# Wide items of 512 columns for v and the first head's q and k, and one weighing for the first four query tiles of a head

## The chip, the cores and the metric

The kernel runs on one core of one Trainium2 chip. The metric is the device time of one execution in microseconds (us); a time is the median of several runs. Five engines work side by side on the core and wait for each other by semaphores: TensorE (PE in the profile; PEld is its weight load), VectorE (DVE), ScalarE (ACT), GpSimd (POOL) and SyncE (SP), whose queue here does nothing but start DMAs. Each engine takes its instructions in the order in which they stand.

## The reference

One decoder layer on 1024 tokens of width 1024, in float32:

```python
h = rms_norm(x, attn_norm_w[l])
proj = h @ w_in[l]
q, k, v, u, g = jnp.split(proj, splits, axis=-1)
# per head: two 64-wide halves of q and k, QK-norm, relative-position bias, causal softmax
p = probs(qb1, k1f) - lamf * probs(qb2, k2f)
return jnp.einsum('bhqk,bhkd->bhqd', p, vf)
# then: per-head norm, convolution branch of width 31 on u, two gated projections,
# x = x + m @ w_out;  x = x + SwiGLU(rms_norm(x))
```

The 8 heads have 128 columns of v each and 128 columns of q and of k each (two halves of 64).

## The kernel before, in words

**Matmuls.** Every float32 product is made of two float32r parts, `hi` (a rounded copy, made by ACT) and `lo` (the remainder, made by DVE or POOL). `mm3` issues three matmuls: hi x hi, hi x lo, lo x hi. A matmul has 128 rows of weights and moves 128, 256, 384 or 512 columns past them; its result lies in PSUM, whose banks hold 512 float32 columns.

**The first stage** (generator `first_stage`) normalises and turns x into `hT_hi`, `hT_lo`, and runs items of the input projection:
- the opening with the first 256 columns of v (V0) and the first convolution chunk U0;
- `first`: V1 and V2, 256 columns of v each. `v_item` takes the weights in two halves of 512 rows (`ld_wide`) and, for a pair of token tiles, fills the two halves of one bank with 24 matmuls of 256 columns each (`gemm_N`);
- seven pairs of convolution chunks (`u_pair`), whose weight sums and token sums POOL prepares;
- `last`: Q0 (q and k of head 0, 128 columns each) and V3 (the last 256 columns of v). `q_item` copies each bank to `qkraw` with ACT, sums the squares of 16 pieces of 64 columns (8 ACT instructions for a bank), makes 1/rms on DVE, scales, and leaves for later (`late`) the turning: PE transposes into a bank pQ, ACT and DVE make the parts `ks`, `klo`, `qs`, and DMAs copy halves of 64 partitions (`turn_qk`).

In the background DVE works through the convolution taps (31 for a chunk, `conv_taps`); ACT makes the first tap of a chunk, copies the finished sum out of PSUM (`done`), and SP writes it to DRAM. `done` and the sums of the chunks 4 to 7 (`acc`) take turns in one buffer of SBUF.

**Attention.** 64 steps (head, query tile) in the order 4, 5, 6, 7, 0, 1, 2, 3 within a head, the last head apart. A step computes scores and softmax (`scores`), turns the weights of the step before into `ph`, `pl` (`turn`), and every second step weighs the values of two query tiles with them (`weigh`, 256 columns in bank pW): for the tiles 2b and 2b+1, 2b+2 key tiles of three matmuls. `back` turns the result. Between them lie pieces of the fill: the items Q1 to Q7 (256 columns) and G0 to G15 (512 columns).

**What sets the order.** The code names what must come after what; within that, a scheduler that simulates the program lays down each engine's order when the kernel is built. So another width of one item moves instructions of all engines around it. The weights come through one stream (`ws`): `ahead` says how many loads are fetched in front. Its split tiles `whi`, `wlo` have three buffers each, the raw tiles `wraw` two. During the first stage `pg` has four banks, in attention two.

Of the kernel before, what the change touches and what calls it, by code (L numbers as in the profile page):

```python
# [13 lines left out]
ALU = mybir.AluOpType  # L14
# [43 lines left out]
def kernel(  # L58
# [284 lines left out]

    class Stream:
# [57 lines left out]
    first = ["V1", "V2"]  # L402
    last = ["Q0", "V3"]
# [12 lines left out]
    def loads_of(it):  # L416
        c = int(it[1:])
        if it[0] == "V":
            return ld_wide(win, [(V0 + 256 * c, 256)])
        if it[0] == "Q":  # L420
            return ld_wide(win, [(Q0 + c * P, P), (K0 + c * P, P)])
        if it[0] == "U":
# [339 lines left out]
    def bias_rows(c0):  # L762
# [6 lines left out]
        pool.dma_start(oh, buckets[:, c0 : c0 + 384])  # L769
# [3 lines left out]
        pool.dma_start(b_d[:, c0 : c0 + 384], gr)  # L773
# [11 lines left out]

    def q_item(h):
        halves = [ws.next(), ws.next()]
        t = {}
        T[h] = t
        for b in (1, 0):  # L790
# [14 lines left out]
            r = rstd_of(ss[:], 16, 1.0 / HD, fast=h > 0)  # L805
            r4 = raw[:].rearrange("p i (g d) -> p (i g) d", d=HD)
            dve.tensor_tensor(r4, r4, r.unsqueeze(2).to_broadcast([P, 16, HD]), op=ALU.mult)

            def turn_qk(z, key, b, raw):


                dma = nc.sync.dma_start
                pt = pm("pQ")
                for i in range(4):
                    pe.transpose(pt[:, i * P : (i + 1) * P], raw[:, i, z * P : (z + 1) * P], ident[:])  # L815
                w = pcol(key + "n")

                def part(j):
                    return qkp.tile([P, 512], F32R, tag=f"{key}s{j}", name=f"{key}s{j}_{h}_{b}", bufs=2 if key == "q" else 3)

                s1, s2 = part(1), part(2)
                act.activation(s1[:], pt[:], AF.Identity, scale=w)
                lo = part(3) if key == "q" else qkp.tile([P, 512], F32R, tag="klo", name=f"klo_{h}_{b}", bufs=1)
                dve.scalar_tensor_tensor(lo[:], pt[:], w, f32(s1[:]), op0=ALU.mult, op1=ALU.subtract)
                if key == "q":
                    dma(f32(s2[HD:, :]), f32(s1[HD:, :]))
                    lo2 = part(4)
                    for one, two in ((s1, s2), (lo, lo2)):
                        if one is lo:
                            dma(f32(two[HD:, :]), f32(one[HD:, :]))  # L830
                        dma(f32(two[:HD, :]), f32(one[HD:, :]))
                        dma(f32(one[HD:, :]), f32(one[:HD, :]))
                    t["q", b] = (s1, lo), (s2, lo2)
                else:
                    act.activation(s2[HD:, :], pt[HD:, :], AF.Identity, scale=w[HD:, :])
                    dma(f32(s2[:HD, :]), f32(lo[HD:, :]))
                    dma(f32(s1[HD:, :]), f32(lo[:HD, :]))
                    t["k", b] = s1, s2

            for z, key in ((1, "k"), (0, "q")):
                free = NT * (h - 1) + (0 if key == "k" and b else NT if key == "q" and not b else NT // 2)
                late.append((free if h else 0, lambda a_=(z, key, b, raw): turn_qk(*a_)))
# [3 lines left out]
    MAKE = {"V": v_item, "U": u_item, "Q": q_item, "G": g_item}  # L848

# [179 lines left out]
    def first_stage():  # L1029
# [13 lines left out]
        for n, _ in enumerate(run(first)):  # L1043
            if n < 5:
                tsum.pop(0)()
            if n == 2:
                ws.ahead = 1
                ws.fetch()
                ws.ahead = 0
# [1085 lines left out]
```

## Time and profile before

| | |
|---|---|
| median of 3 runs | 1727.08 us (1726.94 to 1728.37) |
| span of the profiled execution | 1725.7 us, 25863 instructions |
| busy: PE, PEld | 1714.6 us (99%), 1477.9 us (86%) |
| busy: DVE, ACT, POOL | 1275.4 us (74%), 862.5 us (50%), 219.1 us (13%) |
| V1 and V2 on PE | from 65.27 us to 111.78 us |
| Q0 and V3 begin on PE; first score of attention | 242.67 us; 306.78 us |

The profiled execution has no time of its own beside its span; the median of the runs lies 1.4 us above that span. In rows of groups, "busy" is the time in which at least one of the group's instructions ran, "mean" the duration of one, and matmuls overlap, so the distance from one start to the next is shorter than the duration. The rows of a timeline begin with the start and the duration in us.

### The profile page before, as it was taken

How to read it: one execution, taken by the hardware profiler on the slowest of the kernel's cores; microseconds unless marked ns; L12 is line 12 of the kernel's file. 1: busy time of each engine (PE TensorE's matmuls, PEld its weight loads, DVE VectorE, ACT ScalarE, POOL GpSimd, SP SyncE). 2: the span in 40 equal slices, each digit the busy share in tenths (PEclk: the TensorE clock that was granted, in tenths of full speed). 3: DMA queues.
4: the chain of work that ended last, by engine and by line, in shares of the span. 5: the costliest groups of instructions: out<-in, count | busy, mean ns of one | idle time of the engine just before them, and what ended most of it. 6: DMA issues, size and time to landing. Idle time of an engine off the chain costs nothing.

```text
span 1725.7 us, 25863 instructions
## 1 busy us (share of the span) xinstructions
PE 1714.6 (99%) x9243; PEld 1477.9 (86%) x9243; DVE 1275.4 (74%) x2128; ACT 862.5 (50%) x1958; POOL 219.1 (13%) x207
## 2 busy tenths in 40 slices
PE   9999999999999999999999999999999999999999
PEld 7997889998998998988788888888888888888887
DVE  7675889898988888878687769966676666575544
ACT  5333335767777776756556325633333333333332
POOL 3997851000000000000000000000000000000000
PEclk9999999999999999999999999999999999999999
DMA  6344445336345344343973683245455445598663
GB/s 208 116 126 132 131 151 154 104 109 171 104 127 147 115 125 138 101 136 130 333 238 118 200 296 119 74 135 164 147 170 170 154 141 164 175 355 285 217 215 130
DMA packets 261604, 281.64 MB, mean 163 GB/s; under 512 B 16546, under 2 KB 181986, under 8 KB 261475
## 3 DMA queue, kind: packets, MB, share of 16 engines
q1 hardware_dynamic: 254160, 267.71, 48.3%
q0 software_dynamic: 5680, 9.39, 2.6%
q10 hardware_dynamic: 1634, 2.89, 0.5%
q8 instruction: 73, 1.20, 0.3%
q14 instruction: 57, 0.46, 0.1%
HBM read 181.84 MB, written 85.50 MB: 155 GB/s over the span
## 4 chain that ended last, share of the span: by engine, by line
PE 92%; DMA 3%; DVE 2%; ACT 1%; issue 1%; POOL 0%; SPq 0%; DVEq 0%; POOLq 0%; ACTq 0%
PE acc L980 29%; PE acc L488 12%; PE pg L168 12%; PE pg L169 12%; PE pg L170 12%; PE wo L1850 3%; PE sc L1290 2%; PE sc L1289 2%; PE pT L1328 2%; PE pg L1106 1%; DVE acc L594 1%; PE pW L168 1%; PE pW L169 1%; PE pW L170 1%; PE pQ L815 1%
## 5 line engine op out<-in xcount | busy, mean ns | idle before, releaser
L594 DVE SCALAR_TENSOR_TENSOR acc<-u,cw,acc 128x1023 f32<-128x1023 f32 (+14 forms) x240 | 303.4, 1264 | 23.2 <-ACT acc L588 20.7
L170 PE MATMUL pg<-whi,hT_lo 128*128 128x256 f32 x704 | 200.2, 285 | 0.0
L168 PE MATMUL pg<-whi,hT_hi 128*128 128x256 f32 x704 | 199.7, 285 | 0.4 <-DVE v L125 0.4
L169 PE MATMUL pg<-wlo,hT_hi 128*128 128x256 f32 x704 | 199.5, 284 | 0.0
L125 DVE TENSOR_TENSOR wlo<-draw,whi 128x1024 fp32r<-128x1024 f32 x75 | 91.7, 1223 | 83.4 <-ACT whi L120 78.9
L120 ACT CAST whi<-draw 128x1024 fp32r<-128x1024 f32 x75 | 79.1, 1055 | 129.5 <-PE acc L488 114.3
L169 PEld LDWEIGHTS pg<-wlo,hT_hi 128*128 128x128 f32 x704 | 134.4, 191 | 1.8
L170 PEld LDWEIGHTS pg<-whi,hT_lo 128*128 128x128 f32 x704 | 134.3, 191 | 1.8
L168 PEld LDWEIGHTS pg<-whi,hT_hi 128*128 128x128 f32 x704 | 134.0, 191 | 2.1 <-DVE v L125 0.6
L120 ACT CAST whi<-wraw 128x1024 fp32r<-128x1024 f32 x90 | 94.7, 1052 | 70.6 <-PE pg L169 32.6
L488 PE MATMUL acc<-wlo,whi 128*128 128x512 f32 x308 | 119.8, 389 | 0.0
L488 PE MATMUL acc<-whi,wlo 128*128 128x512 f32 x308 | 119.8, 389 | 0.0
L1296 ACT ACTIVATE E<-E,mn 128x640 f32<-128x640 f32 (+7 forms) x128 | 99.8, 781 | 30.8 <-DVE mn L1291 29.2
L168 PE MATMUL pg<-hT_hi,whi 128*128 128x512 f32 x288 | 114.4, 397 | 0.1
L169 PE MATMUL pg<-hT_lo,whi 128*128 128x512 f32 x288 | 113.7, 395 | 0.0
L170 PE MATMUL pg<-hT_hi,wlo 128*128 128x512 f32 x288 | 113.7, 395 | 0.0
L120 ACT CAST whi<-s 128x1024 fp32r<-128x1024 f32 x54 | 56.9, 1053 | 104.9 <-PE acc L980 101.8
L125 DVE TENSOR_TENSOR wlo<-wraw,whi 128x1024 fp32r<-128x1024 f32 x75 | 93.3, 1246 | 12.6 <-ACT whi L120 12.3
L1291 DVE CUSTOM_DVE_ANT_0 E<-sc,tb 128x512 f32<-128x512 f32 (+3 forms) x128 | 74.2, 585 | 33.2 <-PE pT L1328 16.1
L980 PE MATMUL acc<-h_hi,whi 128*128 128x512 f32 x240 | 93.4, 389 | 0.0
L980 PE MATMUL acc<-h_lo,whi 128*128 128x512 f32 x240 | 93.4, 389 | 0.0
L980 PE MATMUL acc<-h_hi,wlo 128*128 128x512 f32 x240 | 90.1, 389 | 0.0
(370 smaller groups left out, 4589.7 us busy)
## 6 DMA issues: line engine op xcount, KB each, us to landing
wraw<-in_w_gate_up_dram SPq DMA_DIRECT2D x44, 512.0 KB, 4.7
wraw<-in_w_in_dram SPq DMA_DIRECT2D x38, 512.0 KB, 4.0
qs<-qs SPq DMA_DIRECT2D x96, 128.0 KB, 2.3
wd<-in_w_down_dram SPq DMA_DIRECT2D x44, 256.0 KB, 3.1
tdT<-wd SPq DMA_DIRECT2D x88, 128.0 KB, 4.8
draw<-sdS SPq DMA_DIRECT2D x44, 256.0 KB, 3.7
draw<-tdT SPq DMA_DIRECT2D x44, 256.0 KB, 3.7
wraw<-in_w_in_dram SPq DMA_DIRECT2D x32, 256.0 KB, 3.3
```

The lines of the kernel that those rows point to most:

```text
L120: act.copy(dst, src)
L125: last_lo[0] = dve.tensor_tensor(dst, src, f32(hi), op=ALU.subtract).ins
L168: pe.matmul(o, lh, rh, start=start, stop=False)
L169: pe.matmul(o, lh, rl, start=False, stop=False)
L170: last_mm[0] = pe.matmul(o, ll, rh, start=False, stop=stop).ins
L488: m = pe.matmul(o[s_][i][:], l_[:, ts], r_[:, 512:], start=start and j + y_ == 0, stop=j == n - 1 and y_ == 2, skip_group_check=not start,)
L594: dve.scalar_tensor_tensor(a_, us[c][:, : S - n], cw[:, c, t : t + 1], a_, op0=ALU.mult, op1=ALU.add)
L980: last_mm[0] = pe.matmul(o[:], a_[x_][:, k, :], b_[y_][:, k, :], start=start and k + x_ + y_ == 0, stop=k == 3 and x_ == 1, skip_group_che ...
L1289: pe.matmul(o[:, :w], qh[:, qs], k, start=True, stop=False)
L1291: dve.tensor_tensor_reduce(e[:, ks], o[:, :w], tb[:, S - nk + c0 : S - nk + c0 + w], 1.0, mn[:, j : j + 1] if c0 else 3.0e38, ALU.add, ALU ...
L1296: act.activation(e[:, :nk], e[:, :nk], AF.Exp, bias=mn[:, j : j + 1], scale=-1.0, accum_out=l[:, j : j + 1])
L1850: last_mm[0] = pe.matmul(o[s_][i][:], A[u_], B[v_], start=start and j + y_ == 0, stop=j == 3 and y_ == 2, skip_group_check=not start,).ins
```

## The change

V1 and V2 become one item W1 of 512 columns of v; Q0 and V3 become one item W0 of 128 columns of q, 128 of k and 256 of v. A wide item takes its weights in quarters of 256 rows (`ld_quarters`), in the order 0, 1, 2, 3, 0: for four token tiles it holds four banks and goes through the quarters 0 to 3; for the other four through 1, 2, 3, and 0, which is loaded again. Each of the four tiles is taken from its bank after the last quarter. W0 works on the tokens 512 to 1023 first.

In heads 0 to 6 the four query tiles 0 to 3 share one pair `ph`, `pl` with 512 columns, and one `weigh` handles them after tile 3: key tile k for the columns from 128k on, so three matmuls each of 512, 384, 256 and 128 columns in place of 18 of 256. The buffers of `ph` and `pl` are no longer zeroed for these tiles.

The splits of W1's weights go to DVE up to the sixth step (before, POOL took those of V2), and the six DMAs of `bias_rows` go from POOL's queue to SP's.

```diff
+    def ld_quarters(w, cols):
+        def quarter(g):
+            def go():
+                raw = wraw()
+                r3 = raw[:].rearrange("p (k c) -> p k c", c=512)
+                o = 0
+                for c0, n in cols:
+                    nc.sync.dma_start(
+                        r3[:, :, o : o + n],
+                        w[256 * g : 256 * (g + 1), c0 : c0 + n].rearrange("(k p) c -> p k c", p=P),
+                    )
+                    o += n
+                hi, lo = wsplit(raw)
...
+        return [quarter(g) for g in (0, 1, 2, 3, 0)]
...
-    first = ["V1", "V2"]
-    last = ["Q0", "V3"]
+    first = ["W1"]
+    last = ["W0"]
...
+            cols = [(V0 + 256, 512)] if c else [(Q0, P), (K0, P), (V0 + 768, 256)]
+            return ld_quarters(win, cols)
...
-        pool.dma_start(oh, buckets[:, c0 : c0 + 384])
+        nc.sync.dma_start(oh, buckets[:, c0 : c0 + 384])
...
-        pool.dma_start(b_d[:, c0 : c0 + 384], gr)
+        nc.sync.dma_start(b_d[:, c0 : c0 + 384], gr)
...
+    def wide_item(c):
+        def v_parts(i, o, j, n):
+            vh, vl = [t_[:, :n] for t_ in v_tiles[0]()]
+            split_hi(vh, o)
+            split_lo(vl, o, vh)
...
+        w = []
+        for second, b in enumerate((0, 1) if c else (1, 0)):
+            banks = [pg() for i in range(4)]
...
+            for n in range(4):
+                if second and n < 3:
+                    g, (hi, lo) = w[n + 1]
+                else:
+                    ws.ahead = 0 if n == 3 else 1
+                    w.append(ws.next())
+                    g, (hi, lo) = w[-1]
+                for i in range(4):
+                    ts = slice((4 * b + i) * P, (4 * b + i + 1) * P)
+                    o = banks[i]
+                    for k in range(2):
+                        mm3(
+                            o[:], hT_hi[:, 2 * g + k, ts], hT_lo[:, 2 * g + k, ts], hi[:, k, :], lo[:, k, :],
+                            n + k == 0, n == 3 and k == 1,
+                        )
+                    if n < 3:
+                        continue
+                    if c:
+                        v_parts(4 * b + i, o[:], 1, 512)
+                        continue
+                    act.copy(raw[:, i, :], o[:, :256])
...
+                    for y in range(4):
+                        act.activation(
+                            jk, o[:, y * HD : (y + 1) * HD], AF.Square, accum_out=ss[:, 4 * i + y : 4 * i + y + 1]
+                        )
+                    v_parts(4 * b + i, o[:, 256:], 3, 256)
...
+            if c == 0:
+                q_turns(0, b, raw, ss)
+            yield
...
+    def four(h, i):
+        return i < 4 and h < H - 1
...
-        b = i // 2
+        b = 0 if four(h, i) else i // 2
...
+        if four(h, 2 * b):
+            ph, pl = PT.pop((h, 0))
+            for k in range(4):
+                qs = slice(k * P, 512)
+                mm3(o[:, qs], vh[:, k, :], vl[:, k, :], ph[:, k, qs], pl[:, k, qs], k == 0, k == 3)
+            ar = aps.tile([P, 512], F32, tag="at", name=nm("ar"), bufs=2)
+            act.copy(ar[:], o[:])
+            return ar
...
-            if ip % 2:
+            if ip == 3 or ip % 2 and not four(hp, ip):
                 weighs.append((n, (hp, ip // 2)))
```

`q_turns` is the second half of `q_item`, made a function of its own.

**The order around the first score.** On PE before, the last rows ahead of the first score (`sc`) of head 0 are matmuls of Q1 (`pg`, 256 columns); Q0's transposes `pQ` stand some 120 rows further up, and 85 matmuls of Q1 lie ahead of the first score:

```order
L170 MATMUL pg_3287<-whi_2875,hT_lo 128x256
L168 MATMUL pg_3287<-whi_2882,hT_hi 128x256
L1289 MATMUL sc_3163<-ks_0_0_2945,qs_0_1_2778 128x512
L1290 MATMUL sc_3163<-ks_0_0_2945,qs_0_1_2781 128x512
L1289 MATMUL sc_3167<-ks_0_1_2765,qs_0_1_2778 128x128
L1290 MATMUL sc_3167<-ks_0_1_2765,qs_0_1_2781 128x128
```

Now the second pair of `pQ` (tokens 0 to 511 of head 0) stands behind W0 and 77 matmuls of Q1:

```order
L168 MATMUL pg_2959<-whi_2677,hT_hi 128x256
L169 MATMUL pg_2959<-wlo_2678,hT_hi 128x256
L823 MATMUL pQ_2800<-ident,qkraw_2582 128x128 x4
L823 MATMUL pQ_2813<-ident,qkraw_2582 128x128 x4
L170 MATMUL pg_2959<-whi_2677,hT_lo 128x256
L168 MATMUL pg_2959<-whi_2677,hT_hi 128x256
```

After these `pQ` come 61 more matmuls of Q1, of which the last 42 write a third bank, and then the first score. So 138 matmuls of Q1 lie ahead of it.

**ACT at the same place.** Before, the parts of k and q (`ks`, `qs`) stand well ahead of the copy `done` of chunk 3, Q1's first copy and its squares (`jk`), and the first tap `acc` of chunk 4 behind them:

```order
L822 ACTIVATE ks_0_0_2945<-pQ_2940,pvec 128x512
L822 ACTIVATE qs_0_0_2958<-pQ_2953,pvec 128x512
L835 ACTIVATE ks_0_0_2946<-pQ_2940,pvec 64x512
L120 CAST whi_2882<-wraw_2879 128x1024
L120 CAST v_302_3139<-pg_3090 128x512
L1381 ACT_TABLE_LOAD
L276 ACTIVATE lsum<-lsum 128x2
L120 CAST whi_3189<-wraw_3187 128x1024
L598 COPY done_2869<-acc_2405 128x1024
L797 COPY qkraw_3199<-pg_3201 128x512
L800 ACTIVATE jk_3251,ss_319_3200<-pg_3201 128x64 x8
L588 ACTIVATE acc_2972<-u_2403,pvec,cw 128x1024
```

Now `done` and the first tap stand ahead of them:

```order
L623 COPY done_2570<-acc_2235 128x1024
L917 ACTIVATE jk_2759,ss_292_2583<-pg_2580 128x64 x3
L120 CAST v_309_2764<-pg_2580 128x256
L917 ACTIVATE jk_2776,ss_292_2583<-pg_2581 128x64 x4
L120 CAST v_311_2781<-pg_2581 128x256
L677 ACTIVATE t_2789<-v_2786 128x16
L613 ACTIVATE acc_2575<-u_2233,pvec,cw 128x1024
L863 COPY qkraw_2870<-pg_2872 128x512
L866 ACTIVATE jk_2922,ss_327_2871<-pg_2872 128x64 x8
L830 ACTIVATE ks_0_0_2805<-pQ_2800,pvec 128x512
L830 ACTIVATE qs_0_0_2818<-pQ_2813,pvec 128x512
```

The squares of W0's last tiles (`ss_292`) and the root for them (`t`) stand between, and the `ks` of tokens 0 to 511 come last.

**The weighing on PE**, head 0, query tiles 0 and 1 before: six matmuls of 256 columns, followed later by twelve for the tiles 2 and 3:

```order
L1289 MATMUL sc_3969<-ks_1_0_3726,qs_1_1_3709 128x512
L169 MATMUL pW_3885<-pl_3809,vh_3156 128x256
L170 MATMUL pW_3885<-ph_3808,vl_3157 128x256
L168 MATMUL pW_3885<-ph_3808,vh_3156 128x256
L169 MATMUL pW_3885<-pl_3809,vh_3156 128x256
L170 MATMUL pW_3885<-ph_3808,vl_3157 128x256
L1328 MATMUL pT_3945<-ident,E_3821 128x128 x3
```

and now, for all four, at the place of the second group:

```order
L169 MATMUL pW_3735<-pl_3479,vh_2839 128x512
L170 MATMUL pW_3735<-ph_3478,vl_2840 128x512
L168 MATMUL pW_3735<-ph_3478,vh_2839 128x384
L169 MATMUL pW_3735<-pl_3479,vh_2839 128x384
L170 MATMUL pW_3735<-ph_3478,vl_2840 128x384
L168 MATMUL pW_3735<-ph_3478,vh_2839 128x256
L169 MATMUL pW_3735<-pl_3479,vh_2839 128x256
L170 MATMUL pW_3735<-ph_3478,vl_2840 128x256
L168 MATMUL pW_3735<-ph_3478,vh_2839 128x128
L169 MATMUL pW_3735<-pl_3479,vh_2839 128x128
L170 MATMUL pW_3735<-ph_3478,vl_2840 128x128
```

The first group is gone from its place, and one matmul of 512 columns stands some rows above these eleven.

More of the change, by code (lines that the diff above doesn't have):

```diff
@@ L804, in q_item @@
                     yield
[L805 to L844, printed above, removed]
+            q_turns(h, b, raw, ss)
             yield
@@ L1045, in first_stage @@
                 tsum.pop(0)()
[L1046 to L1049, printed above, removed]
-            if n == 4:
+            if n == 5:
+                low_by_pool[0] = True
                 next(ups[0])
                 A = next(ups[0])
-            if n == 5:
                 while tsum:
@@ L1075, in first_stage @@
         ws.ahead = 2
-        yield from run(last[:1])
-        bg.until((NKT - CONV_PSUM) * (CW + 1) - 1)
-        yield from run(last[1:])
+        for n, _ in enumerate(run(last)):
+            if n == 3:
+                bg.until((NKT - CONV_PSUM) * (CW + 1) - 1)
+            yield
     def opening():
@@ L1322, in turn @@
         e = ES.pop((h, i))
-        qs = slice((i % 2) * P, (i % 2 + 1) * P)
+        q0 = i if four(h, i) else i % 2
+        qs = slice(q0 * P, (q0 + 1) * P)
         for k0 in range(0, i + 1, 4):
```

69 lines of the change are left out of this document (62 added, 7 removed).

## The prediction

> **What bounds the kernel now.** I read the page's shares first, then its chain of waits, then the stages that the change touches.
>
> ```profile
> PE 1714.6 (99%) x9243; PEld 1477.9 (86%) x9243; DVE 1275.4 (74%) x2128; ACT 862.5 (50%) x1958; POOL 219.1 (13%) x207
> PE   9999999999999999999999999999999999999999
> PEclk9999999999999999999999999999999999999999
> PE 92%; DMA 3%; DVE 2%; ACT 1%; issue 1%; POOL 0%; SPq 0%; DVEq 0%; POOLq 0%; ACTq 0%
> ```
>
> PE is busy in every slice at full clock, and 92% of the chain that ended last is PE. Whatever shortens PE's stream shortens the kernel, as long as no other engine becomes late. The windows by stage say how much room there is: V1 with V2, Q0 with V3, and attention.
>
> ```profile
> 65.20:111.70 46.50, 46.50 (x388) 46.37 (x387) 31.45 (x30) 15.87 (x19) 44.10 (x21) 1.00 0.39 125
> 242.60:306.70 64.10, 63.74 (x511) 62.52 (x510) 54.34 (x61) 32.16 (x106) 13.60 (x10) 1.00 0.67 185
> 306.70:824.60 517.90, 515.39 (x3423) 470.28 (x3422) 443.50 (x979) 366.87 (x1203) 19.49 (x73) 1.00 0.44 126
> ```
>
> The columns are length, then busy time of PE, PEld, DVE, ACT, POOL, then clock and DMA share. PE has no gap in the first stage, 0.4 us in the second, 2.5 us in attention, where DVE has 74 us to spare (517.9 - 443.5).
>
> **The price of a matmul.** The groups give durations, and these mislead:
>
> ```profile
> L170 PE MATMUL pg<-whi,hT_lo 128*128 128x256 f32 x704 | 200.2, 285 | 0.0
> L168 PE MATMUL pg<-hT_hi,whi 128*128 128x512 f32 x288 | 114.4, 397 | 0.1
> ```
>
> By 285 and 397 ns a wide matmul in place of two narrow ones would save 173 ns. But matmuls overlap; what PE pays is the distance of starts, which the timeline shows where U0 ends and V1 begins, and at V2's end:
>
> ```profile
> 65.04 0.39 PE L170 MATMUL pg<-hT_hi,wlo 128*128 128x512 f32 x1
> 65.27 0.28 PE L168 MATMUL pg<-whi,hT_hi 128*128 128x256 f32 x1
> ...
> 111.66 0.28 PE L170 MATMUL pg<-whi,hT_lo 128*128 128x256 f32 x1
> 111.78 0.40 PE L980 MATMUL acc<-hT_hi,wlo 128*128 128x512 f32 x1
> ```
>
> A wide one takes 0.227 us (65.04 to 65.27). Of the 388 in the stage 384 are V1's and V2's and some two are wide ones of the next item: 46.51 - 2 x 0.23 = 46.05 us for 384, or 0.120 us each. So 256 columns more cost 0.107 us, and 0.013 us goes with each instruction. Two narrow ones take 0.240, a wide one 0.227.
>
> **Part 1, wide items.** V1 and V2: 384 x 0.120 = 46.05 us become 192 x 0.227 = 43.55: 2.5 us less. Q0 and V3 have the same 384: 2.5 us more. Together -5.0 us. On this side the price could only be better if the overhead of 13 ns belonged to the stage, not the instruction, which the rows within U0 exclude.
>
> The Trainium skill ("TensorE: Matmul & The Clock Gate", Back-to-back issue gap) puts the warm gap of a lone stream at N/2.4 + 2.5 ns, 109 and 216 ns here; its per-instruction part is 2.5 ns, not 13, and by it part 1 would give 384 x 2.5 ns = 1.0 us. The 384 matmuls in 46.05 us don't agree with that, and the rows decide.
>
> What part 1 adds lies beside PE. One quarter more is loaded and split for each wide item; DVE takes three splits in W1 and POOL is rid of two.
>
> ```profile
> L120 ACT CAST whi<-wraw 128x1024 fp32r<-128x1024 f32 x5 | 5.2, 1046 | 1.7 <-DMA qs<-qs 1.2 <-issue 0.5
> L125 DVE TENSOR_TENSOR wlo<-wraw,whi 128x1024 fp32r<-128x1024 f32 x75 | 93.3, 1246 | 12.6 <-ACT whi L120 12.3
> ```
>
> A cast is 1.05 us, a subtraction on DVE 1.25. A quarter feeds PE for 24 x 0.227 = 5.4 us, and DVE has 15 us free of 46.5 in the first stage, so this costs nothing unless DVE's taps queue ahead of a split by over 5 us; then each late quarter would cost the rest. The sixteen more DMAs that write v from W1 and bias_rows' six now on SP stand behind loads fetched one item ahead: nothing, or at most the wait of one load, 4 us, if that lead were used up. All four banks of an item end within 4.1 us and are needed again over the next 4.1; in W1 ACT and DVE have one operation each for a bank, which keeps up.
>
> **Part 2, the weighing.** Eighteen matmuls of 256 columns, from 340.70 to 342.86; the prices of 384 and 128 columns come from scores:
>
> ```profile
> 340.70 0.28 PE L168 MATMUL pW<-ph,vh 128*128 128x256 f32 x1
> ...
> 342.74 0.28 PE L170 MATMUL pW<-ph,vl 128*128 128x256 f32 x1
> 342.86 0.27 PE L1328 MATMUL pT<-ident,E 128*128 128x128 f32 x1
> 324.60 0.34 PE L1289 MATMUL sc<-ks,qs 128*128 128x384 f32 x1
> 324.77 0.35 PE L1290 MATMUL sc<-ks,qs 128*128 128x384 f32 x1
> 340.02 0.22 PE L1289 MATMUL sc<-ks,qs 128*128 128x128 f32 x1
> 340.08 0.28 PE L1290 MATMUL sc<-ks,qs 128*128 128x128 f32 x1
> 340.19 0.45 PE L168 MATMUL pg<-hT_hi,whi 128*128 128x512 f32 x1
> ```
>
> 18 x 0.120 = 2.16 us a head. Now 3 x (0.227 + 0.175 + 0.120 + 0.06 to 0.11) = 1.75 to 1.90. Saved: 0.26 to 0.41, and I take 0.37 since 0.06 holds between neighbours of one group; seven heads: -2.6 us (-1.8 to -2.9). It counts in full only while PE sets attention's pace. The copies of pW and the zeroing get fewer on ACT and POOL, which have room.
>
> **Part 3, the seam before attention.** Before, Q0 was turned while V3 ran. Now k and q of tokens 0 to 511 come out of W0's very end, and the first score needs them. PE fills in with Q1. Call W0's last matmul T. Without a wait the order gives 77 x 0.120 = 9.2 us to pQ, 0.8 for eight transposes, 61 x 0.120 = 7.3: first score at T + 17.3. The rows of the chain:
>
> ```profile
> 277.31 1.03 PE L815 MATMUL pQ<-ident,qkraw 128*128 128x128 f32 x8
> 278.10 0.36 PE L169 MATMUL pg<-wlo,hT_hi 128*128 128x256 f32 x1
> 304.58 0.23 ACT L800 ACTIVATE jk<-pg 128x64 f32<-128x64 f32 x1
> 304.93 0.22 ACT L800 ACTIVATE jk<-pg 128x64 f32<-128x64 f32 x1
> L797 ACT COPY qkraw<-pg 128x512 f32<-128x512 f32 x5 | 2.9, 583 | 8.9 <-PE pg L170 8.8
> L1342 ACT COPY ar<-pW 128x256 f32<-128x256 f32 x32 | 11.9, 372 | 19.4 <-PE pW L170 19.3
> L822 ACT ACTIVATE ks<-pQ,pvec 128x512 fp32r<-128x512 f32 x2 | 1.4, 680 | 1.2 <-PE pQ L815 1.2
> 286.39 0.17 DVE L657 TENSOR_TENSOR r<-r,t 128x16 f32<-128x16 f32 x1
> 287.70 1.22 DVE L807 TENSOR_TENSOR qkraw<-qkraw,r 128x1024 f32<-128x1024 f32 x1
> 302.97 1.01 ACT L598 COPY done<-acc 128x1024 f32<-128x1024 f32 x1 [3.76 <-DVE acc L594]
> 310.61 1.24 ACT L588 ACTIVATE acc<-u,pvec,cw 128x1024 f32<-128x1024 f32 x1 [3.29 <-DMA c_d<-done]
> DMA to landing us min/median/max: 4.3/4.8/6.6
> ks<-klo SPq DMA_DIRECT2D x32, 128.0 KB, 2.4
> ```
>
> A square with its read takes 0.35 us (304.58 to 304.93). Each of W0's last four tiles costs ACT 0.37 + 4 x 0.35 + 0.37 = 2.1 us, while PE delivers one every 1.1 us from T - 3.4. With one `ks` (0.7), one split (1.05) and `done` (1.0) between, ACT is through at T + 7.9; root, five small DVE operations and the scaling (0.2 + 0.9 + 1.2) end at T + 10.2. PE stands at pQ from T + 9.2: 1.0 us lost.
>
> Behind the root ACT now has chunk 4's first tap, which waits until `done` is in DRAM, as the row at 310.61 shows; before, Q1's copy and squares stood ahead of it. `done` ends at about T + 4.7, lands 4.3 to 6.6 us later, the tap takes 1.2, Q1's copy and squares 3.4: T + 13.6 to 15.9. Only then is a bank free for Q1's third group, which PE reaches at 10.2 + 0.8 + 2.3 = T + 13.3. With 42 x 0.120 = 5.0 us behind, the first score is at T + 18.6 to 20.9, so 1.3 to 3.6 us late; at the median landing (4.8) 1.8. The `ks` (0.7 + 0.7), its low part on DVE (0.75) and the DMA (2.4) are ready about 1 us earlier and hide. I take 2.0 (1 to 4); a gain is excluded, since PE's order is fixed.
>
> Against that stands a wait of V3 that has no place in W0, where the banks come free in the order of need:
>
> ```profile
> 298.04 0.39 PE L168 MATMUL pg<-whi,hT_hi 128*128 128x256 f32 x1 [0.36 <-DVE v L125]
> ```
>
> So 0.4 us goes (0 to 0.4).
>
> **Sum.** -5.0 - 2.6 - 0.4 + 2.0 = -6.0 us: span 1725.7 to 1719.7. The median lies 1.4 us over the span, so 1727.1 becomes 1721.1. T is at 242.67 - 2.5 + 24 x 0.227 + 43.55 + 0.8 = 290.0, the first score at 309.3 in place of
>
> ```profile
> 306.78 0.40 PE L1289 MATMUL sc<-ks,qs 128*128 128x512 f32 x1
> ```
>
> **Rivals.**
>
> *Attention is held by the vector side (slower).* 138 matmuls of Q1 instead of 85 lie ahead of the first score, so attention has 53 x 0.120 = 6.4 us less fill, and 2.6 less weighing: PE must pass it in 509 us in place of 518 with the same DVE and ACT work. If scores, softmax and turning set the pace, attention keeps its 517.9 us and only starts 2.5 us later: 1727.1 + 2.5 = 1729.6, and 1731 with the slow landing. It decides from the point where PE would idle more than 9 us there. Against it: 2.5 us idle today, DVE 86% busy; for it: the chain from score to turned weights is not in these shares.
>
> *Waits of k and q eat half (no change).* Two scores in attention wait for DMAs today, 1.1 us for `ks` and 0.8 for `qs`:
>
> ```profile
> PE sc L1289 <- DMA ks<-klo: 1.1, 1, 1.1
> PE sc L1290 <- DMA qs<-qs: 0.8, 1, 0.8
> ```
>
> With less weighing ahead, four of the seven remaining heads might meet such a wait: +4.4, so 1725.5.
>
> *A wide matmul costs what two narrow ones do*, 0.240: part 1 gives nothing, the rest -2.6 - 0.4 + 2.0, so 1726.1. The rows of U0 speak against it. The skill's 2.5 ns, named above, would come near this.
>
> *More than forecast*: the seam hides behind Q1 and those two waits go too: -5.0 - 2.9 - 0.4 - 1.9 = -10.2, so 1716.9.
>
> **Chances.** Forecast 0.66, with a range of its own of 1719 to 1723.8 (seam 1 to 4, weighing -1.8 to -2.9, the lost wait 0 to 0.4, rarely all at one end); vector side 0.12; waits 0.16; no gain from width 0.02; more 0.04. A measurement of this kernel tells 0.2%, 3.5 us, from no change: faster is under 1723.6, slower over 1730.5. Faster: 0.63 of the forecast, 0.04 of the waits' case at its mild end, and the last case, 0.71 in all, cut to 0.68 because seven heads of reordered attention hold more than I listed. Slower: half of the vector case and that reserve, 0.09. Same: the rest, 0.23. For 8 in 10 the range reaches up through the waits' case, to 1727, and down to 1717.5.
>
> **What would show it.** V and Q stages: 192 wide matmuls 0.227 apart, W1 from 65.3 to about 108.8; at another distance part 1 is wrong. Seam: PE idle at pQ and at Q1's third group, released by DVE and ACT, first score near 309; at 312 or later the landing was worse than any seen. Attention: PE's idle time stays near 2.5 us and the stretch from first score to its end falls to about 509 us; if it stays at 518, the vector side holds it. Eleven of the twelve pW matmuls of a head should take 1.6 us or less.

## The result, and the profile after

The changed kernel takes 1743.91 us (median of 4 runs, 1741.45 to 1745.20), the kernel before in the same comparison 1727.01: 1.0098 times as long (95% interval 1.0084 to 1.0111). It is slower by 17 us; 6 us less were forecast. The profiled execution has a span of 1742.6 us, 16.9 more than the one before, and its page says:

```profile
PE 1717.6 (99%) x8817; PEld 1461.0 (84%) x8817; DVE 1286.2 (74%) x2135; ACT 864.4 (50%) x1961; POOL 211.1 (12%) x172
PE   9999999999999999999899999999999999999999
PEclk9999999999999999999899999999999999999999
PE 89%; DVE 4%; DMA 4%; ACT 1%; issue 1%; SPq 0%; POOL 0%; DVEq 0%; ACTq 0%
```

PE has 426 matmuls fewer and is busy for 3 us more. In slice 20 its work and its granted clock both dip, which they did nowhere before, and the chain now has 4% each of DVE and DMA. The windows by stage of the kernel after (length, busy time of PE, PEld, DVE, ACT, POOL, clock, DMA share, GB/s) are W1; the convolution pairs; W0 and Q1 up to the first score; attention up to the last matmul of its fill; the attention projection:

```profile
65.80:109.90 44.10, 43.89 (x193) 35.96 (x193) 36.62 (x31) 16.27 (x20) 40.31 (x19) 1.00 0.36 119
109.90:243.80 133.90, 131.34 (x571) 105.72 (x570) 102.98 (x96) 51.15 (x70) 100.22 (x62) 1.00 0.43 132
243.80:314.90 71.10, 69.04 (x371) 60.17 (x371) 60.91 (x71) 38.13 (x138) 17.46 (x12) 0.98 0.67 190
314.90:827.90 513.00, 507.39 (x3317) 461.16 (x3316) 436.89 (x970) 357.33 (x1168) 13.26 (x44) 0.99 0.43 123
827.90:932.90 105.00, 98.45 (x424) 78.97 (x423) 68.83 (x128) 55.24 (x91) 0.00 (x0) 0.95 0.70 241
```

The same of the kernel before, for the stages that the prediction did not show in these bounds:

```profile
111.70:242.60 130.90, 130.80 (x571) 105.40 (x570) 99.51 (x93) 50.89 (x69) 102.15 (x67) 1.00 0.42 127
306.70:822.60 515.90, 513.39 (x3415) 468.63 (x3414) 441.79 (x978) 365.09 (x1198) 19.49 (x73) 1.00 0.44 125
822.60:916.30 93.70, 92.68 (x422) 75.99 (x421) 67.49 (x125) 51.95 (x86) 0.00 (x0) 1.00 0.79 269
```

From the starts of the matmuls at these bounds, what was forecast and what came:

| stage | forecast | measured |
|---|---|---|
| opening | 0 | +0.6 (between -0.4 and +1.2 in the other kernels below, none of which touches it) |
| V1, V2 as W1 | -2.5 | -2.5 |
| convolution pairs | 0 | +3.1 |
| W0 and Q1 up to the first score (-2.5 - 0.4 + 2.0 + 6.4) | +5.5 | +7.0 |
| attention (-6.4 - 2.6) | -9.0 | -2.9 |
| attention projection | 0 | +11.3 |
| all behind it | 0 | +0.3 |
| sum | -6.0 | +16.9 |

Two thirds of the loss lie in a stage that the prediction does not mention. What PE waited for, in the whole program (us in total, times, longest); shown are the waits of 0.9 us and more that the kernel before does not have at that length:

```profile
PE sc L1367 <- DVE mn L1369: 2.6, 3, 1.8
PE pg L168 <- ACT whi L120: 2.4, 1, 2.4
PE pg L168 <- DVE v L125: 2.1, 1, 2.1
PE pS L1462 <- DVE an L1455: 1.9, 1, 1.9
PE acc L1062 <- POOL wlo L131: 1.7, 1, 1.7
PE pW L168 <- DMA vh<-v_hi: 1.2, 1, 1.2
PE pW L170 <- DMA vl<-v_lo: 0.9, 1, 0.9
```

**The half clock.** The waits alone do not make up the loss. Windows laid where the granted clock changes, and behind them two rows of PE's timeline:

```profile
296.58:300.00 3.42, 3.42 (x18) 3.42 (x18) 1.52 (x3) 3.26 (x18) 0.00 (x0) 0.50 0.84 223
402.40:409.22 6.82, 5.86 (x27) 5.28 (x26) 4.67 (x8) 3.70 (x12) 0.41 (x2) 0.50 0.54 162
832.48:835.89 3.41, 1.35 (x8) 0.92 (x9) 2.09 (x7) 0.42 (x2) 0.00 (x0) 1.00 0.62 198
835.89:842.72 6.83, 6.03 (x17) 4.53 (x16) 4.51 (x7) 5.24 (x8) 0.00 (x0) 0.50 0.99 337
846.13:849.54 3.41, 1.03 (x5) 0.67 (x4) 0.82 (x1) 3.38 (x5) 0.00 (x0) 1.00 1.05 405
849.54:852.96 3.42, 3.42 (x9) 2.38 (x8) 1.54 (x2) 0.10 (x1) 0.00 (x0) 0.50 0.99 344
```

```profile
841.50 0.63 PE L168 MATMUL pg<-aTh,whi 128*128 128x512 f32 x1
841.93 0.63 PE L169 MATMUL pg<-aTl,whi 128*128 128x512 f32 x1
```

The clock is granted by stretches of 3.41 us. After one in which PE was idle for 2.06 us (3.41 - 1.35) the next two have the clock at 0.50, after one with 2.38 us the next; there a matmul of 512 columns starts every 0.43 us (841.50 to 841.93) in place of 0.227. The four rows at 0.50 are all there are: 20.5 us with 18.7 us of PE's work in them (3.42 + 5.86 + 6.03 + 3.42). Of each 0.43 us 0.20 is lost, so by this estimate they cost about 18.7 x 0.47 = 9 us of the 16.9. The Trainium skill ("TensorE: Matmul & The Clock Gate", What's actually happening) describes it: a window of 3413 ns that runs freely, and half the clock after an idle one. The trace agrees in length and in the factor of two. The rule of thumb of the Trainium skill on the same page (Why this matters for your kernels), to avoid gaps of over about 3 us, does not suffice here: single waits of 2.06 us (for a bank at the end of W0) and 2.38 us were enough.

### The profile page after: what moved, and what is told of

Read it like the earlier page. It is cut to its first block, busy times and chain, and to the rows that moved or that the text cites. A ratio compares the mean times of both kernels' runs of the same rounds, so it can differ in the third digit from the quotient of the medians.

```text
span 1742.6 us, 24998 instructions
## 1 busy us (share of the span) xinstructions
PE 1717.6 (99%) x8817; PEld 1461.0 (84%) x8817; DVE 1286.2 (74%) x2135; ACT 864.4 (50%) x1961; POOL 211.1 (12%) x172
## 4 chain that ended last, share of the span: by engine, by line
PE 89%; DVE 4%; DMA 4%; ACT 1%; issue 1%; SPq 0%; POOL 0%; DVEq 0%; ACTq 0%
PE acc L1062 29%; PE acc L513 12%; PE pg L168 11%; PE pg L169 11%; PE pg L170 11%; PE wo L1948 3%; PE sc L1368 2%; PE sc L1367 2%; DVE acc L619 2%; PE pT L1413 2%; PE pg L1185 1%; PE pW L170 1%; PE pW L169 1%; PE pW L168 1%; DMA vl<-v_lo 1%
## 5 line engine op out<-in xcount | busy, mean ns | idle before, releaser
L168 PE MATMUL pg<-whi,hT_hi 128*128 128x256 f32 (+1 forms) x576 | 177.7, 310 | 2.3 <-DVE v L125 2.1
L169 PE MATMUL pg<-wlo,hT_hi 128*128 128x256 f32 (+1 forms) x576 | 178.2, 309 | 0.0
L170 PE MATMUL pg<-whi,hT_lo 128*128 128x256 f32 (+1 forms) x576 | 177.4, 309 | 0.0
L125 DVE TENSOR_TENSOR wlo<-wraw,whi 128x1024 fp32r<-128x1024 f32 x78 | 100.8, 1293 | 24.4 <-ACT whi L120 23.4
L168 PEld LDWEIGHTS pg<-whi,hT_hi 128*128 128x128 f32 x576 | 110.0, 191 | 9.8 <-DVE v L125 2.5
L170 PEld LDWEIGHTS pg<-whi,hT_lo 128*128 128x128 f32 x576 | 110.0, 191 | 6.2
L169 PEld LDWEIGHTS pg<-wlo,hT_hi 128*128 128x128 f32 x576 | 110.0, 191 | 6.2
```

Source lines behind the costliest of these rows:

```text
L125: last_lo[0] = dve.tensor_tensor(dst, src, f32(hi), op=ALU.subtract).ins
L168: pe.matmul(o, lh, rh, start=start, stop=False)
L169: pe.matmul(o, lh, rl, start=False, stop=False)
L170: last_mm[0] = pe.matmul(o, ll, rh, start=False, stop=stop).ins
```

## The experiments

Each was timed against the kernel before in five rounds. The ratio is to the kernel before.

**1. The look-ahead set back.** The windows show the attention projection 11.3 us longer. The second weight of that projection came late. ACT and PE of the kernel after:

```profile
845.16 2.59 ACT L1731 ACTIVATE gt<-gt 128x512 f32<-128x512 f32 x4 [3.86 <-DMA gt<-g_d]
847.66 1.98 ACT L120 CAST whi<-wraw 128x1024 fp32r<-128x1024 f32 x2
848.74 0.50 PE L168 MATMUL pg<-aTh,whi 128*128 128x512 f32 x1 [2.38 <-ACT whi L120]
```

Before, it was split ahead of the last transposes:

```profile
824.62 1.05 ACT L120 CAST whi<-wraw 128x1024 fp32r<-128x1024 f32 x1
```

In the order of PE the last transposes `pS` stand behind 52 matmuls of the projection before, behind 15 now. The cause is a state: `wide_item` sets `ws.ahead = 0` at its last quarter. Behind W1 it is set anew, behind W0 it is not, so that all of attention loads and splits a weight only when its item asks for it, where Q0 and V3 left it at 2. Late was the split, not the load: SP issues no load of this projection's weights between 799.60 and 849.98 us, and the two casts at 847.66 us stand behind the gates `gt` in ACT's order.

```diff
             if n == 3:
                 bg.until((NKT - CONV_PSUM) * (CW + 1) - 1)
             yield
+        ws.ahead = 2
```

> The whole change, and one line more: behind W0 the look-ahead of the weight stream is set back to 2. W0 sets it to 0 at its last quarter and nothing sets it back, so that from there on a weight is only fetched when its item asks for it; before, Q0 and V3 left it at 2. Theory L (the loss of 11.3 us between the last matmul of attention's fill and the first one of the convolution projection comes from this: the second weight of the attention projection was not there, so PE had 15 matmuls instead of 52 to put in front of the last transposes): that stretch falls from 105 us to 94 to 98, time 1733 to 1737. Rival V (attention's vector side is too slow for less fill, and the end is only its last effect): nothing changes, 1743 to 1745.

1737.51 us, 1.0057 (1.0044 to 1.0069): 6.4 us better than the whole change, and the stage takes 95.4 us in place of 105. L holds for the stage; the total misses its range by 0.5 us. 10.6 us are left for other causes.

**2 to 4. Each part alone.**

The weighing alone (the loads and `bias_rows` as before too):

```diff
-    first = ["W1"]
-    last = ["W0"]
+    first = ["V1", "V2"]
+    last = ["Q0", "V3"]
```

> Only the weighing of four query tiles together; V1, V2, Q0 and V3 stay narrow, and their order of loads too. The prediction's part 2: seven times 0.37 us less, 1724.4. Rival E (the order at the end: with this part alone 30 matmuls of the attention projection stand ahead of the last transposes, before 52, so PE comes there 22 x 0.227 = 5.0 us earlier, where it had about 4.7 us to spare): the gain goes there, 1726 to 1728. Rival V (fewer matmuls of its own leave attention to the vector side): 1727 and PE idle by 2.6 us more in attention.

W1 alone:

```diff
-    last = ["W0"]
+    last = ["Q0", "V3"]
...
-        return i < 4 and h < H - 1
+        return False
```

> Only W1 is wide; Q0 and V3 are narrow, each head is weighed in two groups. Theory Q (the sixteen writes of W1's second half stand in SP's queue ahead of the loads of the second convolution pair, which land 4 to 5 us late): -2.5 for the wide matmuls, +2.9 for the wait at the first convolution pair, 1727.4. The prediction's part 1, which put this wait at nothing: 1724.5.

W0 alone (the same with `first = ["V1", "V2"]` and their loads as before):

> Only W0 is wide (it leaves the look-ahead at 0); V1 and V2 are narrow, each head is weighed in two groups. The prediction: -2.5 for the wide matmuls, -0.4, +2.0 for the seam, 1726.1. Theory L: the end of attention loses 5 to 11 us as in the whole change, and the seam with its wait of 2.1 us and the half clock behind it takes 1 to 4 more than predicted: 1732 to 1740.

| alone | time | ratio (95%) | stages against before |
|---|---|---|---|
| weighing | 1736.61 | 1.0054 (1.0040 to 1.0067) | attention +6.0, projection +2.2 |
| W1 | 1728.11 | 1.0007 (0.9998 to 1.0016) | W1 -2.5, convolution pairs +2.7 |
| W0 | 1742.13 | 1.0087 (1.0073 to 1.0101) | to the first score +5.5, attention -5.9, projection +13.2 |

W0 alone has the seam at the very price forecast (+5.5), though by another wait (2.06 us for a bank), and attention gives back 5.9 of the 6.4 us of fill that went ahead of it. What it loses is in the projection, more than L had put there, so that the total is 2.1 us over L's range. PE waits there 4.1 us for one weight, and 10.2 us are at half clock. 30 matmuls stand ahead of the last transposes, as many as with the weighing alone, which loses 2.2 us there: what costs is less their number than the late weight. W1 alone gives 2.5 us in its stage and loses 2.7 in the next, as Q said; its total is 0.7 us over Q's. The weighing, forecast at -2.6, costs 9.7: both E and V fell short there.

**5. W1 with the next loads first.** SP's queue after, and before:

```profile
114.21 2.25 SPq L886 DMA_DIRECT2D v_lo<-u  x2
116.56 1.04 SPq L1026 DMA_DIRECT2D wraw<-in_w_in_dram  x2
```

```profile
108.86 0.41 SPq L944 DMA_DIRECT2D wraw<-in_w_in_dram  x1
```

The loads of the second convolution pair start 7.7 us later, behind sixteen writes of v that take SP from 106.64 to 116.5 us. Some of them wait for DVE, which makes the low part of a token tile between two convolution taps; but nearly every write also holds SP for 0.3 to 0.5 us by itself.

```diff
                         v_parts(4 * b + i, o[:], 1, 512)
+                        if second and i == 1:
+                            hook.pop()()
...
+        def second_pair():
+            next(ups[0])
+            next(ups[1])
+
+        hook.append(second_pair)
...
-            if n in (6, 7):
+            if n == 6:
                 next(ups[0])
...
-            next(ahead)
+            if c > 1:
+                next(ahead)
```

> Only W1 wide, as in the run before, and the two loads of the second convolution pair issued in the middle of W1's second half, ahead of the last eight writes of v. Theory Q (those loads stood behind sixteen writes that wait for DVE, one after another): PE no longer waits 0.5 and 1.7 us at the first convolution pair, the stretch of the convolution pairs falls from 133.5 us to 131, time 1725.0 to 1725.8. Rival (POOL's and ACT's own order makes the parts late, not the load): no change, 1728.

1726.19 us, 0.9994 (0.9985 to 1.0003). The loads start at 110.28, and the convolution pairs cost +1.1 in place of +2.7. Q holds for most of it. The total misses its range by 0.4 us: the first score now comes 6.3 us earlier than before, and PE waits there (experiment 11).

**6. W0 with the look-ahead set back.**

> Only W0 wide, with the look-ahead set back to 2 behind it. Theory L (the second weight of the attention projection was fetched too late): the stretch from attention's last fill matmul to the convolution projection falls from 107 us to 94, no half clock there, time 1728 to 1730. Rival (W0 itself leaves attention's end short of work in another way): 1740 to 1743 as without the line. If L holds, what is left over 1726.9 is the price of the seam.

1727.27 us, 1.0002 (0.9993 to 1.0011): 14.9 us better than without the line. The attention projection without the line, and with it:

```profile
821.70:928.60 106.90, 99.47 (x423) 79.18 (x422) 71.65 (x130) 56.67 (x94) 0.00 (x0) 0.95 0.69 236
```

```profile
823.10:915.80 92.70, 92.24 (x423) 76.37 (x422) 67.73 (x126) 51.73 (x86) 0.00 (x0) 1.00 0.76 268
```

L is settled; the total is 0.7 us below its range. W0 itself then costs 0.5 us, within the uncertainty of nothing.

**7. Moved, not merged.**

```diff
-            for k in range(4):
-                qs = slice(k * P, 512)
-                mm3(o[:, qs], vh[:, k, :], vl[:, k, :], ph[:, k, qs], pl[:, k, qs], k == 0, k == 3)
+            for c0, nk in ((0, 2), (256, 4)):
+                qs = slice(c0, c0 + 256)
+                for k in range(nk):
+                    mm3(o[:, qs], vh[:, k, :], vl[:, k, :], ph[:, k, qs], pl[:, k, qs], k == 0, k == nk - 1)
```

> As the run with the weighing alone, but the four query tiles are weighed with the 18 matmuls of 256 columns of before, all at the new place: moved, not merged. Theory P (the six matmuls that stood two steps earlier were cover there, and their place is what costs): attention has the same waits on DVE, ACT and the DMA of k, and 2.1 us more of PE's own work: 1736 to 1739.5. Rival W (the place is harmless; it is the smaller work of PE that the vector side cannot follow): 1726.5 to 1729.

1733.93 us, 1.0043 (1.0031 to 1.0056). That lies in neither range. All 18 matmuls are there and it still loses 7 us, so the move costs, not the width. That it is 2.7 us faster than the merged one, with 2.1 us more to do, P did not expect, and its waits are others: behind head 0, from 394 to 400 us, PE waits 2.9 us in three places, with 6.8 us of half clock from 396.9 us on. With the place the move changes the round of banks (experiments 13 and 14) and how long `ph` and `pl` are held; no run parts these. Merging itself does what it should. Of one merged weighing, PE's rows:

```profile
380.54 0.40 PE L168 MATMUL pW<-ph,vh 128*128 128x512 f32 x1
382.80 0.40 PE L169 MATMUL pW<-pl,vh 128*128 128x512 f32 x1
384.32 0.27 PE L170 MATMUL pW<-ph,vl 128*128 128x128 f32 x1
384.43 0.45 PE L1371 MATMUL sc<-ks,qs 128*128 128x512 f32 x1
```

Eleven matmuls in 1.63 us (382.80 to 384.43) and one of 0.23: 1.86 us in place of 2.16, 0.30 saved a head.

**8. Both wide items with three repairs**: the hook of experiment 5, the line of experiment 1, and

```diff
-                            jk, o[:, y * HD : (y + 1) * HD], AF.Square, ...
+                            jk, raw[:, i, y * HD : (y + 1) * HD], AF.Square, ...
```

> W1 and W0 wide, each head weighed in two groups, with three repairs: the loads of the second convolution pair ahead of the last writes of W1, the look-ahead set back to 2, and the squares of W0 taken from the copy in SBUF in place of the bank, so that a bank comes free 1.4 us earlier. If the losses are the three that the runs before named: -2.5 for W1, -2.5 for W0, +1 to 3 at the seam, about as much PE idle in attention as before: 1721 to 1726. If the seam's price stays (2.1 us for a bank and 1.6 of half clock): 1725 to 1728.

1728.38 us, 1.0010 (1.0001 to 1.0019). The third repair failed: PE waited 2.9 us for the bank in place of 2.1, and the first score came 3.3 us later against W0's start than in experiment 12, which lacks it. In the repaired run ACT's copy of the third bank (292.33 us) stands behind a `ks` that waits 2.15 us for DVE; in experiment 12 that `ks` does not wait. At the first score PE then waits 1.5 us for ACT, where in experiment 12 it waited 0.5 us for a DMA. Why the order came out so is open.

**9. The weighing for heads 2 to 6.** In attention PE waits in experiment 2 for

```profile
PE pg L168 <- ACT jk L866: 3.3, 2, 2.7
PE sc L1371 <- DMA ks<-klo: 2.6, 1, 2.6
PE sc L1371 <- DVE mn L1373: 2.5, 3, 1.7
```

The largest two of ACT's and DVE's stand together at 393 to 398.5 us, behind head 0's weighing, with 3.4 us of half clock behind them. ACT copied a bank of Q2 at 382.40 and took its squares only at 395.69, after softmax work that had to wait:

```profile
382.40 0.59 ACT L863 COPY qkraw<-pg 128x512 f32<-128x512 f32 x1 [1.44 <-PE pg L170]
389.54 1.05 ACT L120 CAST whi<-wraw 128x1024 fp32r<-128x1024 f32 x1 [3.40 <-PE pg L170]
395.69 0.25 ACT L866 ACTIVATE jk<-pg 128x64 f32<-128x64 f32 x1
```

Before, the squares of that bank follow its copy at once:

```profile
384.34 0.59 ACT L797 COPY qkraw<-pg 128x512 f32<-128x512 f32 x1
384.80 0.25 ACT L800 ACTIVATE jk<-pg 128x64 f32<-128x64 f32 x1
```

So the move has changed ACT's order as well: with the squares further down, ACT stood idle for 3.4 us ahead of the cast at 389.54. In experiment 7 the copy is at 385.70 and the squares begin at 395.62. The six moved matmuls are 0.7 us of work, less than PE waits here. Whether lost cover or the new order of ACT costs more, no run shows.

```diff
-        return i < 4 and h < H - 1
+        return i < 4 and 1 < h < H - 1
```

> The weighing alone as in the run with it, but only for the heads 2 to 6; heads 0 and 1 are weighed in two groups. Theory S (one place: behind head 0's weighing PE comes to six pairs of scores with no fill between and waits 1.7 and 2.7 us, with half clock behind): attention loses 6 us less, and gains 5 x 0.3; with the 2.2 us at the end, where still 30 matmuls stand ahead of the last transposes, 1727 to 1729. Rival H (every head so weighed loses about 1 us by waits): 1732 to 1735.

1732.69 us, 1.0039 (1.0026 to 1.0051). By the total H would be right, but the stages say S: attention is 1.0 us shorter than before where seven heads made it 6.0 longer, and PE waits in it only 1.5 us for the DMA of `ks` and 0.4 us for DVE. The rest is lost behind attention (+3.2 in the projection, +2.0 up to the FFN), more than the 2.2 us that both theories had put there.

**10. No blocks of zeros, nothing moved.**

```diff
-            mm3(o[:, :256], vh[:, k, :], vl[:, k, :], ph[:, k, :], pl[:, k, :], k == 0, k == nkt - 1)
+            qs = slice(P if k == nkt - 1 else 0, 256)
+            mm3(o[:, qs], vh[:, k, :], vl[:, k, :], ph[:, k, qs], pl[:, k, qs], k == 0, k == nkt - 1)
```

> The kernel before, with one edit: each weighing leaves out the block of zeros (its last key tile weighs only the later query tile, 128 columns in place of 256, and the buffers are not zeroed). Nothing is moved, so the cover stays. If three matmuls of 128 columns cost 0.29 us as in the merged weighing, against 0.36: 0.07 x 32 = 2.2 us less, 1724.6 to 1725.5. Rival (the weight load sets the pace of such a matmul, or what is saved turns into waits): 1726.5 to 1727.5.

1732.16 us (1729.33 to 1738.18), 1.0030 (1.0020 to 1.0040): worse than either theory. PE waits 1.9, 1.7 and 1.5 us in attention (for `ar`, `qs` and `jk`), where it waited 1.1 and 0.8 us before (for `ks` and `qs`); the profiled run is the fastest of nine, so that the other 3 us are not shown. The cause is open.

**11. More fill ahead of the first score** (on experiment 5):

```diff
+        if n == 0:
+            more(2)
-        scores(h, i)
+        with after(last_fill[0] if n == 0 else None):
+            scores(h, i)
         scm.append(last_mm[0])
-        more((p + 1) // 2)
+        if n > 1:
+            more((p + 1) // 2)
```

> W1 wide with its loads first, and the first score held behind the first 96 matmuls of Q1 (51 without this, 85 before); the pieces of Q1 that are spent there are taken from the first two steps of attention. Theory F (the first score came too early: PE waits 1.4 us for DVE, 1.3 us for ACT, and the half clock that follows takes 1.6 more): these 4.3 us go, time 1722 to 1724. Rival (the first two steps of attention now lack the fill, and the waits only move): 1725.5 to 1728.

1724.22 us, 0.9986 (0.9977 to 0.9995): faster than both kernels, and 0.2 us over F's range. F is half right: the wait for DVE is gone, but in the profiled run the one for ACT grew,

```profile
PE pg L168 <- ACT jk L866: 2.5, 1, 2.5
```

with the half clock behind it still there. That run, at 1728.57, is the slowest of the eleven.

**12. Both wide items, without the third repair.**

> W1 and W0 wide with W1's loads first and the look-ahead set back to 2, each head weighed in two groups; the squares of W0 are taken from the bank again. From the runs with each alone: -0.6 for W1 with its loads first, +0.4 for W0 with the look-ahead: 1725.5 to 1727.5. If the squares from the copy were what made the seam worse in the repaired run (3.1 us for a bank in place of 2.2, first score 3.5 us later), this run has its first score 3 us earlier than that one and is 1.5 to 3 us faster than it; if not, both are equal at 1728.4.

1726.93 us, 0.9998 (0.9989 to 1.0007), 1.5 us faster than with the third repair, as expected (the two intervals just overlap). Both wide items together are worth nothing measurable. It also shows when a wait halves the clock:

```profile
289.96:293.37 3.41, 2.38 (x11) 1.65 (x9) 3.41 (x6) 3.28 (x16) 0.00 (x0) 1.00 0.88 228
293.37:296.79 3.42, 2.40 (x20) 2.40 (x21) 2.19 (x3) 3.36 (x15) 0.00 (x0) 1.00 1.04 247
337.74:341.16 3.42, 1.67 (x13) 1.39 (x13) 3.42 (x9) 1.65 (x4) 0.00 (x0) 1.00 0.20 77
```

The bank's wait of 2.05 us at W0's end falls on two stretches, 1.0 us in each, and the clock stays; in the whole change the same wait of 2.06 us fell into one, and the clock was halved.

**13, 14. The round of banks.** The small products `pW`, `pB`, `pT`, `pS`, `pQ` draw their PSUM banks from a list of three in turn. A head weighed at once draws one fewer. Orders built for several sets of heads have 52 or 53 matmuls of the projection ahead of the last transposes with 0, 3 or 6 such heads, and 30 with 1, 4, 5 or 7. Run were three heads and six (`h < 6`), the weighing alone as in experiment 2:

```diff
-        return i < 4 and h < H - 1
+        return i < 4 and 1 < h < 5
```

> The weighing alone, for the heads 2, 3 and 4. Theory B: the banks of the small products go round by three, and a head weighed at once draws one bank fewer; with three such heads the round is as before, 52 matmuls of the attention projection stand again ahead of the last transposes (30 with five or with seven heads), and the end loses nothing. Then 1726.9 - 3 x 0.3 = 1726, within 0.7. Rival (the end's loss goes with the heads weighed at once, not with the round of banks): 1729 to 1731.

> The weighing alone, for the heads 0 to 5: again a multiple of three, 52 matmuls ahead of the last transposes. Theory B and theory S together: attention loses about 6 us as with seven heads, the end nothing: 1732 to 1734, against 1736.6 with seven heads. Rival to B: 1736 to 1737.

Three heads: 1727.58 us, 1.0007 (0.9998 to 1.0016). Six: 1735.09, 1.0047 (1.0035 to 1.0060). The projection with six heads, and with seven (experiment 2):

```profile
828.60:921.90 93.30, 92.49 (x421) 76.06 (x421) 67.28 (x126) 51.83 (x86) 0.00 (x0) 1.00 0.79 270
```

```profile
828.90:924.80 95.90, 93.45 (x421) 75.86 (x420) 69.16 (x129) 56.58 (x93) 0.00 (x0) 1.00 0.79 265
```

B holds for the end (-0.4 against before, and +0.5 with three heads). The totals are 0.9 and 1.1 us over the ranges: with three heads what was saved went into one wait of 2.6 us for the DMA of `ks`, 1.1 us before, with 3.4 us of half clock behind it.

**15, 16. The parts put together.** Experiment 11 with the heads 2 to 4 weighed at once, and experiment 12 with the same; the edit is that of experiment 13.

> The fastest run so far (W1 wide with its loads first, the first score behind 96 matmuls of Q1) with the weighing at once for the heads 2, 3 and 4, 52 or 53 matmuls ahead of the last transposes. By B: 1724.2 - 0.9 = 1723.3, faster than both kernels. If every edit to attention brings waits of its own: 1725 to 1729.

> All three parts of the change with their repairs: W1 wide with its loads first, W0 wide with the look-ahead set back to 2, the weighing at once for the heads 2, 3 and 4. By the runs with the parts: 1726.9 (both wide) - 0.9 = 1726. If the parts disturb each other in attention: 1728 to 1732.

1725.34 us, 0.9990 (0.9981 to 0.9998), and 1727.31, 1.0004 (0.9995 to 1.0013). The first is faster than both kernels but no better than experiment 11: the 0.9 us did not come, as the rival said. The whole change with its repairs is back at the time of before, 1.3 us over what was expected. The 0.9 us were worked out from PE's rows: the run with three heads itself had shown no gain (1.0007), and with it the parts as measured give what came (0.9998 x 1.0007 = 1.0005, and 0.9986 x 1.0007 = 0.9993).

## Why the prediction was wrong

The forecast was 1721.1 with a range up to 1727.0; it is 1743.9. By the runs the 17 us are, roughly, 9.7 for the weighing (alone), 6.4 for the look-ahead, 1.2 for W1, 0.5 for W0: 17.8, within 1 us. That they add up so well is in part luck: the look-ahead is worth 6.4 us beside the weighing, but 14.9 where W0 is alone (experiments 4 and 6). The weighing loses at the end of attention too; how the two losses meet there was not followed up.

- **The price of a matmul** was right: 0.227 us for 512 columns (W1's first two rows, below, and 44.1 us for its stage, where 44.0 were forecast with the two rows behind it).

```profile
65.84 0.39 PE L168 MATMUL pg<-whi,hT_hi 128*128 128x512 f32 x1
66.06 0.39 PE L169 MATMUL pg<-wlo,hT_hi 128*128 128x512 f32 x1
```

- **Part 1's cover** is the first step that failed: "the sixteen more DMAs that write v from W1 ... nothing, or at most the wait of one load, 4 us, if that lead were used up". I took nothing; it was 3.1 us, and eats W1's gain. The lead was used up because the sixteen writes hold SP's queue for 9.8 us, by their issuing and by waits for DVE (experiment 5). DVE's splits took 2.2 to 2.7 us each in W1, not the 1.25 us that were read off attention, and cost PE nothing there.
- **The end of attention** is the step that is missing. The prediction followed the seam and the weighing and took the rest of the program as it was. What came there was +11.3 us: the split of the second weight comes late, since W0 leaves the look-ahead at 0 (experiments 1 and 6). The order that the schedule lays down at 828 us had already changed: 15 matmuls ahead of `pS` for 52. It could have been read; only the two places that the change touches were looked at. The state `ws.ahead = 0` stands in the diff.
- **Part 2** saved 0.30 us a head by itself, where 0.37 (0.26 to 0.41) was taken. What failed is "it counts in full only while PE sets attention's pace" with the answer that it does. A loss from the new place was not among the bounds, which went from -1.8 to -2.9. Without any saving the move costs 7 us (experiment 7), most of it behind head 0 and about 1 us in the projection; merged, the end loses 2 to 5. That the moved matmuls were cover at their old place is one reading; the changed order of ACT is the other, and the cause stays open between them. In the whole change head 1's v came late as well (the 1.2 and 0.9 us above, with 6.8 us of half clock behind them). Its load is issued where head 0's weighing ends, at 389.7 us, and is needed at 402.1, 12.4 us later; before, these were 383.0 and 405.3, with 22.3 us between. And `vl` took 13.4 us to land, by the chain of waits, for 7.4 before.
- **Part 3** was right in size by luck, and wrong in its chain. T came at 293.7, the first score at 314.94, T + 21.2 for 18.6 to 20.9 (T + 20 in the runs with W0 alone). Of the two waits that were forecast, at pQ and at Q1's third group, neither came. Left out was that Q1's first group needs one of the four banks that W0 still holds:

```profile
295.94 0.39 PE L168 MATMUL pg<-whi,hT_hi 128*128 128x256 f32 x1 [2.06 <-DVE v L125]
314.94 0.40 PE L1367 MATMUL sc<-ks,qs 128*128 128x512 f32 x1
```

"A wait of V3 that has no place in W0" was therefore wrong: it came back nearly six times as long, with half clock behind it.

- **The rivals.** "Attention is held by the vector side" named a slower outcome, but not this one: with W0 alone attention fell by 5.9 of the 6.4 us. "Waits of k and q" was seen as a wait of 2.6 us for `ks` with the weighing alone, for seven heads and for three, not in the change. None priced a wait above its own length, though the half clock that followed four times was about 9 of the 16.9 us.

## What to carry to other kernels

Where a schedule is laid down by simulation, an edit changes it everywhere: compare the two orders at each place where little work lies ahead of a chain (the ends of stages above all), not only where the edit is, and look for states that new code leaves behind (a look-ahead, a round of banks, a place in a queue). Matmuls that are saved by moving them can cost more than they save (0.3 us a head against 7 us for the move here): look at what every engine does at the old place and at the new one. A wait of PE of 2 us is to be priced at about 3.6 us (2 + 3.41 x 0.47, an estimate from the rows above) where it falls into one stretch of the clock.

## What was not expected of the hardware

In the eleven traces that show a halved clock ahead of the kernel's end its stretches lie on a grid of 3.41 us. Laid on that grid (the first and the last 25 us left out), a stretch at full clock in which PE was idle for 1.94 us or more was followed by half clock 11 times in 11; with 1.34 to 1.81 us it happened in some and not in others (1.75 us did both); with 1.32 us or less never. Experiment 16 has half clock only at its very end, from 1723.84 us on; on the grid laid back from there, 1.83 us (3.42 - 1.59) were not followed by it:

```profile
290.23:293.65 3.42, 1.59 (x7) 0.97 (x6) 3.42 (x5) 3.33 (x15) 0.00 (x0) 1.00 0.93 262
293.65:297.06 3.41, 3.19 (x26) 3.19 (x27) 1.82 (x3) 3.32 (x15) 0.00 (x0) 1.00 1.03 236
```

A stretch at half clock was followed by another where PE was idle in it for 0.69 to 1.02 us, not where it was under 0.3 us. So waits in a row count together, and two waits of the same length cost differently by where they fall.
